# A decoder trunk on one core: the first tile's modulation split between TensorE and VectorE, its turned halves in two banks, the small rows turned later

## The chip, the cores and the metric

The kernel runs on one core of one Trainium2 chip. The metric is the device time of one execution in microseconds (us); three timed executions of the kernel before took 685.24, 685.53 and 686.24 us, so the median is 685.53 us.

## The reference

One decoder layer (`DEPTH = 1`) works on `x` of 512 rows by 1024 columns. What matters here is its head: a modulation is computed from a vector `c`, `x` is normalised and modulated, and the result is multiplied by the wide matrix `w_in`.

```python
cs = jax.nn.silu(c)
mod = cs @ w_ada[l] + b_ada[l]
shift1, scale1, gate1, shift2, scale2, gate2 = ...
h = _rmsnorm(x, norm1_g[l]) * (1.0 + scale1) + shift1
proj = h @ w_in[l]
qa, ka, va, qd, kd, vd, ga, gd = jnp.split(proj, points, axis=-1)
...
```

Behind it come a sliding-window attention, a differential attention, gates, an output projection and a gated MLP with a short convolution. All of that is the same in both kernels, in fp32 made of pairs of a rounded high part and a rest ("hi" and "lo").

## The kernel before, in words

**Layout.** `x` is held as `xn`, four tiles of 128 rows. `h` is needed transposed, as eight "k tiles" of 128 channels by 512 positions: `hTh[k]` (high part) and `hTl[k]` (rest). For every k tile the first stage needs a column pair `mods[k]` (scale and shift for 128 channels), which is a product of the vector `cs` with two 1024 by 128 slices of `w_ada` (`adaw[k]`, with `j` = 0 for the scale and 1 for the shift, and `kk` = 0..7 for the rows in groups of 128). It also needs 128 rows of `w_in` (768 columns, `w0[k]`), split into `w0h` and `w0l`. Six accumulators `acc6[0..5]`, one PSUM bank each, collect the products over the eight k tiles: per tile 6 x (`w0h` x `hTh`), 6 x (`w0l` x `hTh`) and 6 x (`w0h` x `hTl`).

**The head of the program.** `crow8` (the vector `c`) and `rows` (parts of `b_ada`, `norm1_g`, and `diff_subln_g`) are loaded and turned on TensorE; `rows` becomes `cols`, a column of biases and gains. TensorE runs filler products (`keep_warm(n)`: n blocks of 128 columns, products of ones with ones) while it waits. ScalarE squares the four tiles of `x` (`stat`), VectorE makes the reciprocal roots (`root`, which writes `rst`), the first 256 columns of each tile are scaled (`normalise` on VectorE for tiles 0 and 1, `scale_head` on ScalarE for 2 and 3), and `turn(t)` transposes the 128 columns of the first k tile into the bank `xt0`. Tile 0's modulation is summed from five products on TensorE (`direct0`, `kk` 0..4) and from three multiply-adds on VectorE (`add_a0`, `kk` 5..7, into `a0[j]`), which a last product with ones adds up. `finish_mod(0)` makes `mods[0]`; `h_tile(0)` writes `hTh[0]`, and the product of tile 0 begins.

**The eight tiles.** The loop over `gi` computes tile `gi`'s products on TensorE and, beside them, prepares tile `gi + 1`: `split_hi` on ScalarE, `ac_ops` on VectorE (the modulation sums), `reduce_mod`, `h_turn`, `finish_mod` (its shift column is written by ScalarE, line 337), `h_tile` on ScalarE (line 383: first `hTh`, then the same in fp32, `hf`), `h_low` on VectorE.

**What sets the order.** The loads of this stage lie in the SP queue in the order of the text: `x`, then `adaw` and `w0` of tile after tile, then four small loads (`sink`, `lamv`, `crow` twice), then the weights of the next stage: `w768_0`, `w1280_0` and so on, in 512 KB pieces (`load_cols`, line 567). Each engine runs its own instructions strictly in the order in which they are placed. Within `manual_schedule`, VectorE, ScalarE and TensorE keep the order of the text; instructions that are written behind that block are placed by a scheduler, by its own estimate of times, and it may put them in front of instructions of the block. Two such instructions of the next stage are the casts `w768_0_h` and `w1280_0_h` (line 128, `split`, called by `load_cols`), each 128 x 1024 on ScalarE.

Of the kernel before, what the change touches and what calls it, by code (L numbers as in the profile page):

```python
# [8 lines left out]
F32 = mybir.dt.float32  # L9
# [5 lines left out]
P = 128  # L15
D = 1024
S = 512
# [30 lines left out]
WARM_EARLY = 5  # L48
WARM = 8
# [11 lines left out]
def kernel(  # L61
# [104 lines left out]
    nc.sync.dma_start(crow8, c.rearrange("o (a p) -> (o a) p", p=P))  # L166
    NR = 16 + 8 + 1
# [3 lines left out]
    nc.scalar.dma_start(rows[24:25, :], diff_subln_g)  # L171
    crow = cpool.tile([88, P], F32, name="crow")
# [51 lines left out]
    def load_ada(k):  # L224
        if k % 3 == 2:
            aw = big.tile([P, 2, KT, P], F32, tag="out" + "hl"[k // 3], name=f"adaw{k}")
        else:
            aw = pp.tile([P, 2, KT, P], F32, tag="adaw", bufs=2, name=f"adaw{k}")
        cut = 4 if 0 < k < 5 else KT
        for a in range(0, KT, cut):  # L230
            for j, base in ((0, D), (1, 0)):
# [11 lines left out]
    with tc.manual_schedule(engines={nc.sync.engine}):  # L243
        for t in range(NT):
            nc.sync.dma_start(xn[:, t], xd[t * P : (t + 1) * P, :])
# [10 lines left out]
        nc.sync.dma_start(crow[66:88, :], conv_b[0].rearrange("(a p) -> a p", p=P))  # L256

# [10 lines left out]
    pc = tbank("pc", (P, NR))  # L268


    keep_warm(WARM_EARLY)
    nc.tensor.transpose(pc, rows, ident[:NR, :NR])
    cols = cpool.tile([P, NR], F32, name="cols")
    nc.vector.tensor_copy(cols, pc)
    bsh, bsc1, n1g, sublnc = cols[:, 0:8], cols[:, 8:16], cols[:, 16:24], cols[:, 24:25]
    nc.vector.tensor_scalar_add(bsc1, bsc1, 1.0)
    nc.vector.tensor_scalar_mul(n1g, n1g, -0.5)
    nc.vector.tensor_scalar_mul(sublnc, sublnc, -0.5 * (1.0 - LAM_INIT))
# [25 lines left out]
    def direct(pa, j, k, kks, start=True, stop=False):  # L304
        for kk in kks:
            nc.tensor.matmul(
                pa[:, j],
                adaw[k][:, j, kk],
                cs[:, kk : kk + 1].to_broadcast([P, P]),
                start=start and kk == kks[0],  # L310
                stop=stop and kk == kks[-1],
            )

    def early_mod(gi):
        pa = tbank(f"pa{gi}", (P, 2, P))
        direct(pa, 0, gi, (6, 7))
        return pa

    def reduce_mod(gi, early=None):
        pa = early or tbank(f"pa{gi}", (P, 2, P))  # L320
        for j in range(2):
            if early:
                if j:
                    direct(pa, 1, gi, (6, 7))
                nc.tensor.matmul(pa[:, j], ac[gi][0][:, j], ones, start=False, stop=True)
            else:
                nc.tensor.matmul(pa[:, j, 0:1], ac[gi][0][:, j], ones[:, 0:1], start=True, stop=True)
        return pa

    def finish_mod(k, pa):  # L330
        pa = pa if k == 0 else [pa[:, 0], pa[:, 1]]
        m = pp.tile([P, 16], F32, tag="mod", bufs=3, name=f"mod{k}")
        last = nc.vector.scalar_tensor_tensor(
            m[:, 0:1], pa[0][:, 0:1], bsc1[:, k : k + 1], n1g[:, k : k + 1], ALU.add, ALU.mult
        )
        if k:
            nc.scalar.activation(m[:, 1:2], pa[1][:, 0:1], AF.Identity, bias=bsh[:, k : k + 1])
        else:
            nc.vector.tensor_add(m[:, 1:2], pa[1][:, 0:1], bsh[:, k : k + 1])
        mods[k] = m  # L340
        return last
# [33 lines left out]
    def h_turn(k):  # L375
        pts[k] = tbank(f"xt{k}")
        for t in range(NT):
            nc.tensor.transpose(pts[k][:, t * P : (t + 1) * P], xn[:, t, k * P : (k + 1) * P], ident)

    def h_tile(k, between=None):  # L380
        hf = pp.tile([P, S], F32, tag="hf", bufs=2, name=f"hf{k}")
        for dst in (hTh[k], hf):
            nc.scalar.activation(dst, pts[k], AF.Identity, bias=mods[k][:, 1:2], scale=mods[k][:, 0:1])
# [11 lines left out]
    def mm_k(k, part, some=DONE):  # L395
# [4 lines left out]
        for i in some:  # L400
            for p in (1, 2) if last and part else (0, 1) if part == 0 and not last else (part,):
                lhs, rhs = ((wh, hTh), (wl, hTh), (wh, hTl))[p]
                nc.tensor.matmul(
                    acc6[i], lhs[:, i * P : (i + 1) * P], rhs[k], start=k == 0 and p == 0, stop=last and p == 2
                )
# [23 lines left out]
    pts[0] = tbank("xt0")  # L429

    def turn(t):
        nc.tensor.transpose(pts[0][:, t * P : (t + 1) * P], xn[:, t, 0:P], ident)
# [6 lines left out]
    DIRECT = 5  # L439

    def add_a0(j, kks):
        for kk in kks:
            w, f = adaw[0][:, j, kk], cs[:, kk : kk + 1]
            if kk == DIRECT:
# [4 lines left out]
    def direct0(j):  # L449
        for kk in range(DIRECT):  # L450
            nc.tensor.matmul(
                pa0[j], adaw[0][:, j, kk], cs[:, kk : kk + 1].to_broadcast([P, P]), start=kk == 0, stop=False
            )
# [16 lines left out]
    direct0(0)  # L470
    turn(2)
    direct0(1)
    for j in range(2):
        nc.tensor.matmul(pa0[j], a0[j], ones, start=False, stop=True)
    turn(3)
    finish_mod(0, pa0)
    split_hi(0, 0)
    keep_warm(2)
# [3 lines left out]
    for gi in range(KT):  # L482
# [20 lines left out]
        if gi == 0:  # L503
            h_turn(1)
        mm_k(gi, 0, DONE if gi else FIRST[:5])
        mm_k(gi, 1)
        if more:
            if gi == 0:
                split_lo(1, 0)
            pa = reduce_mod(gi + 1, early_mod(1) if gi == 0 else None)  # L510
            if gi == 0:
                mm_k(0, 0, FIRST[5:])
            if ALONE <= gi + 2 < KT:
# [5 lines left out]
            if gi:  # L519
                split_lo(gi + 1, 0)  # L520
# [38 lines left out]
    pcv = tbank("pcv", (P, 88))  # L559
    nc.tensor.transpose(pcv, crow, ident[:88, :88])  # L560
    cv = cpool.tile([P, P], F32, name="cv")
    nc.vector.tensor_copy(cv[:, :88], pcv)
# [1497 lines left out]
```

## Time and profile before

| what | value |
|---|---|
| median of three timed runs | 685.53 us (685.24 to 686.24) |
| profiled execution, first to last instruction (span) | 684.1 us |
| what lies around the span, against the median | 1.43 us |
| PE (TensorE) busy | 675.3 us, 99% |
| DVE (VectorE), ACT (ScalarE) busy | 564.2 us, 384.5 us |
| first product of tile 0 starts | 15.36 us |

The page gives the profiled execution's span; its own time, with the launch and the end around it, is not on the page, and is taken here as the span plus the 1.43 us by which the median exceeds it.

In the rows of a timeline, the first number is the start in us, the second the busy time in us, then the engine (PEld is TensorE's weight load, SPq the SP queue as it issues transfers), the line, the operation, output <- inputs, the shape and the count; brackets give the time for which the engine was idle before and what ended that. A row that holds several instructions starts with the first of them.

### The profile page before, as it was taken

What the parts mean: (1) busy time and instruction counts of PE and PEld (TensorE: products, weight loads), DVE (VectorE), ACT (ScalarE), POOL (GpSimd) and SP (SyncE); (2) the same over time, 40 slices, a digit from 0 to 9 for tenths busy, and PEclk for the clock granted to TensorE, in tenths of its full rate; (3) what the DMA queues carried; (4) which work ended last, traced back from release to release, by engine and by line L of the source; (5) the groups of instructions that cost most, each with busy time, mean ns of one, the idle gap of its engine ahead of it and who ended that gap; (6) DMA issues with size and microseconds to landing.
All of it is one profiled execution on the core that took longest, in us unless ns stands there. A gap on an engine that the chain in (4) does not pass through costs nothing. (4 is left out here: it accounts for less than half of the span.)

```text
span 684.1 us, 11125 instructions
## 1 busy us (share of the span) xinstructions
PE 675.3 (99%) x4141; PEld 589.7 (86%) x4141; DVE 564.2 (82%) x1075; ACT 384.5 (56%) x688; POOL 98.5 (14%) x119
## 2 busy tenths in 40 slices
PE   9999999999999999999999999999999999999995
PEld 5887887878888888888899999999999998888885
DVE  4999875988796756974589988888888999979997
ACT  6776774546543223324377665666555665656765
POOL 3000000011012012021030111112120003440300
PEclk9999999999999999999999999999999999999999
DMA  9995422565456885659555788777978647995903
GB/s 304 349 296 181 144 62 64 163 166 162 144 157 181 255 246 158 217 144 345 187 93 109 170 216 212 180 165 207 216 194 216 153 170 186 191 205 146 166 1 123
DMA packets 117142, 123.89 MB, mean 181 GB/s; under 512 B 5063, under 2 KB 94184, under 8 KB 117088
## 3 DMA queue, kind: packets, MB, share of 16 engines
q1 hardware_dynamic: 97246, 95.11, 43.3%
q0 software_dynamic: 19648, 27.79, 24.1%
q8 instruction: 32, 0.52, 0.3%
q10 hardware_dynamic: 194, 0.28, 0.1%
q14 instruction: 22, 0.18, 0.1%
HBM read 118.97 MB, written 2.11 MB: 177 GB/s over the span
## 5 line engine op out<-in xcount | busy, mean ns | idle before, releaser
L1362 PE MATMUL up<-t,m_whi 128*128 128x256 f32 x512 | 93.1, 283 | 0.0
L1362 PEld LDWEIGHTS up<-t,m_whi 128*128 128x128 f32 x512 | 79.9, 192 | 0.0
L1362 PE MATMUL up<-t,m_wlo 128*128 128x256 f32 x256 | 72.4, 283 | 0.0
L1362 PE MATMUL up<-bh,p_whi 128*128 128x256 f32 x232 | 65.7, 283 | 0.0
L1362 PE MATMUL up<-bl,p_whi 128*128 128x256 f32 x232 | 65.7, 283 | 0.0
L1362 PE MATMUL up<-bh,p_wlo 128*128 128x256 f32 x232 | 65.7, 283 | 0.0
L952 POOL DMA_DIRECT2D arow<-arow x28 | 22.5, 804 | 247.8 <-DVE sd L821 123.6
L1362 PEld LDWEIGHTS up<-t,m_wlo 128*128 128x128 f32 x256 | 49.2, 192 | 0.0
L1271 POOL DMA_DIRECT2D s<-in_w_up_dram x21 | 26.9, 1353 | 141.3 <-DMA s<-in_w_up_dram 69.2
L1362 PEld LDWEIGHTS up<-bh,p_whi 128*128 128x128 f32 x232 | 44.5, 192 | 0.0
L1362 PEld LDWEIGHTS up<-bl,p_whi 128*128 128x128 f32 x232 | 44.5, 192 | 0.0
L1362 PEld LDWEIGHTS up<-bh,p_wlo 128*128 128x128 f32 x232 | 44.5, 192 | 0.0
L944 DVE SCALAR_TENSOR_TENSOR arow<-ra,cs,arow 128x512 f32<-128x512 f32 x56 | 41.8, 748 | 0.6
L1299 ACT CAST m_whi<-s 128x1024 fp32r<-128x1024 f32 x31 | 32.4, 1046 | 11.1 <-DVE s L1293 6.3
L1303 DVE TENSOR_TENSOR m_wlo<-s,m_whi 128x1024 fp32r<-128x1024 f32 x31 | 37.8, 1218 | 0.0
L1362 PE MATMUL up<-t,p_whi 128*128 128x256 f32 x176 | 32.2, 283 | 0.0
L1362 PEld LDWEIGHTS up<-t,p_whi 128*128 128x128 f32 x176 | 27.5, 192 | 0.0
L816 ACT ACTIVATE sd<-sd,dmx 128x128 f32<-128x128 f32 (+3 forms) x32 | 17.7, 557 | 17.3 <-DVE dmx L806 17.3
L1369 ACT ACTIVATE gT<-a,cv 128x512 f32<-128x512 f32 x22 | 17.7, 813 | 16.9 <-DVE a L1404 15.8
L1299 ACT CAST p_whi<-wa 128x1024 fp32r<-128x1024 f32 x18 | 18.7, 1041 | 12.6 <-PE up L1362 12.6
L1303 DVE TENSOR_TENSOR p_wlo<-wa,p_whi 128x1024 fp32r<-128x1024 f32 x18 | 22.0, 1222 | 3.8 <-ACT p_whi L1299 3.8
L1362 PE MATMUL up<-t,p_wlo 128*128 128x256 f32 x88 | 24.9, 283 | 0.0
(499 smaller groups left out, 2052.4 us busy)
## 6 DMA issues: line engine op xcount, KB each, us to landing
ra<-in_w_ada_dram SPq DMA_DIRECT2D x32, 512.0 KB, 4.9
wa<-in_w_up_dram SPq DMA_DIRECT2D x22, 512.0 KB, 4.2
s<-in_w_up_dram SPq DMA_DIRECT2D x21, 512.0 KB, 4.7
s<-in_w_up_dram POOLq DMA_DIRECT2D x21, 512.0 KB, 6.9
w<-in_w_in_dram SPq DMA_DIRECT2D x12, 512.0 KB, 5.0
a<-in_w_up_dram SPq DMA_DIRECT2D x11, 512.0 KB, 4.7
b<-in_w_down_dram SPq DMA_DIRECT2D x10, 512.0 KB, 4.2
adaw<-in_w_ada_dram SPq DMA_DIRECT2D x8, 512.0 KB, 6.3
```

Of the source, the lines that this page charges most:

```text
L816: exp = nc.scalar.activation(pm[m], pm[m], AF.Exp, bias=mx[:, m : m + 1], scale=slope, accum_out=ls)
L944: nc.vector.scalar_tensor_tensor(ac, r[:, a], cc, ac, ALU.mult, ALU.add)
L952: nc.gpsimd.dma_start(whole[0:n], whole[n : 2 * n], accum_op=ALU.add)
L1271: nc.gpsimd.dma_start(dst, upblock(*blk), accum_op=ALU.add)
L1299: nc.scalar.copy(W[J, name][0], R[J, SRC[name]])
L1303: nc.vector.tensor_sub(lo, R[J, SRC[name]], hi.bitcast(F32))
L1362: nc.tensor.matmul(o[u], w[:, k, cu], b[:, k], start=name in ("p1", "m5", "p2") and k == 0 and x == 0, stop=k == 3 and x == 2, skip_group_ ...
L1369: nc.scalar.activation(grow(j), av[J][:, u], AF.Identity, bias=cv[:, 66 + j : 67 + j], scale=cv[:, 44 + j : 45 + j])
```

## The change

Seven edits, all in the first stage:

1. The load of `c` goes from the SP queue to ScalarE's queue, ahead of the small rows; `diff_subln_g` is no longer a row of `rows`; it is loaded behind `crow` by the SP queue and turned with `crow` (89 rows in place of 88).
2. `adaw[0]` is loaded in four pieces of 256 KB in place of two of 512 KB.
3. The filler products of 5 and 8 blocks (with the turn of `rows` between them) become one run of 25 blocks ahead of the first turn of `x`. The single block behind the second turn and the two blocks before the first product are gone.
4. `rows` is turned behind the second turn of `x` (`turn_rows`), into the bank of `acc6[3]`; VectorE's copy into `cols` stands ahead of `root(2)`.
5. Tile 0's modulation: TensorE takes `kk` 0..5 of the scale and 2..7 of the shift, VectorE the other two of each.
6. Tile 0's turned columns lie in two banks; VectorE writes the first half of `hTh[0]`, ScalarE the second.
7. In the products of tile 0, all `w0h` products come ahead of the `w0l` ones; the products for tile 1's modulation are put together and their sums placed behind the products of `acc6[5]`; `split_lo(1, 0)` moves behind `finish_mod(1)`.

```diff
-WARM_EARLY = 5
-WARM = 8
+WARM = 25
...
-    nc.sync.dma_start(crow8, c.rearrange("o (a p) -> (o a) p", p=P))
+    nc.scalar.dma_start(crow8, c.rearrange("o (a p) -> (o a) p", p=P))
...
-        cut = 4 if 0 < k < 5 else KT
+        cut = 4 if k < 5 else KT
...
+        nc.sync.dma_start(crow[88:89, :], diff_subln_g)
...
-    keep_warm(WARM_EARLY)
-    nc.tensor.transpose(pc, rows, ident[:NR, :NR])
...
+    def turn_rows():
+        pc = acc6[3][:, :NR]
+        nc.tensor.transpose(pc, rows, ident[:NR, :NR])
+        nc.vector.tensor_copy(cols, pc)
+        nc.vector.tensor_scalar_add(bsc1, bsc1, 1.0)
+        nc.vector.tensor_scalar_mul(n1g, n1g, -0.5)
...
         for dst in (hTh[k], hf):
-            nc.scalar.activation(dst, pts[k], AF.Identity, bias=mods[k][:, 1:2], scale=mods[k][:, 0:1])
+            for src in pts[k]:
+                q = slice(src[1], src[1] + src[0].shape[-1])
+                if k == 0 and dst is not hf and src[1] == 0:
+                    nc.vector.tensor_scalar(dst[:, q], src[0], mods[k][:, 0:1], mods[k][:, 1:2], ALU.mult, ALU.add)
+                else:
+                    nc.scalar.activation(
+                        dst[:, q], src[0], AF.Identity, bias=mods[k][:, 1:2], scale=mods[k][:, 0:1]
+                    )
...
         if t in (1, 2):
             normalise(t - 1)
             turn(t - 1)
-            keep_warm((4, 1)[t - 1])
+            if t == 1:
+                keep_warm(4)
+                direct0(0, range(4), True)
+    turn_rows()
     root(2)
-    add_a0(0, range(DIRECT, DIRECT + 2))
+    add_a0(0, (6,), 6)
     root(3)
-    add_a0(0, range(DIRECT + 2, KT))
-    add_a0(1, range(DIRECT, KT))
+    add_a0(0, (7,), 6)
+    add_a0(1, (0, 1), 0)
     scale_x(0)
     scale_head(2)
     scale_head(3)
     scale_x(1)
-    direct0(0)
+    direct0(0, (4, 5))
+    direct0(1, (2, 3), True)
     turn(2)
-    direct0(1)
-    for j in range(2):
-        nc.tensor.matmul(pa0[j], a0[j], ones, start=False, stop=True)
+    sum0(0)
     turn(3)
-    finish_mod(0, pa0)
+    direct0(1, range(4, KT))
+    sum0(1)
...
-    keep_warm(2)
+    h_turn(1)
```

Where the instructions stand changes in the head, as the text says, and in one place that the text doesn't show.

TensorE in the head, from the filler products (`a5<-ones`) to the last products of tile 0's modulation; before, from the filler run to the first five products of the scale:

```order
L184 MATMUL a5_113<-ones_67 128x512
L184 MATMUL a5_113<-ones_67 128x128
L272 MATMUL pc_193<-ident_69,rows_103 128x25
L184 MATMUL a5_113<-ones_67 128x512 x2
L432 MATMUL xt0_205<-ident_69,xn_123 128x128
L184 MATMUL a5_113<-ones_67 128x512
L432 MATMUL xt0_205<-ident_69,xn_123 128x128
L184 MATMUL a5_113<-ones_67 128x128
L451 MATMUL pa0_206<-cs_188,adaw0_130 128x128 x5
```

and in the changed kernel:

```order
L182 MATMUL a5_112<-ones_67 128x512 x6
L182 MATMUL a5_112<-ones_67 128x128
L441 MATMUL xt0_204<-ident_69,xn_122 128x128
L182 MATMUL a5_112<-ones_67 128x512
L459 MATMUL pa0_205<-cs_190,adaw0_129 128x128 x4
L441 MATMUL xt0_204<-ident_69,xn_122 128x128
L275 MATMUL a3_114<-ident_69,rows_103 128x24
L459 MATMUL pa0_205<-cs_190,adaw0_129 128x128 x2
L459 MATMUL a4_110<-cs_190,adaw0_129 128x128 x2
L441 MATMUL a5_112<-ident_69,xn_122 128x128
L465 MATMUL pa0_205<-ones_67,a0_0_206 128x128
L441 MATMUL a5_112<-ident_69,xn_122 128x128
```

Ahead of the first turn of `xn` stand 25 filler blocks without a break in place of 13 with the turn of `rows` in them, and the turn of `rows` now follows the second turn of `xn`, behind four products of the modulation.

ScalarE near the end of the first stage, from the last part of tile 7's modulation (`ac7`) over tile 6's shift column and transposed tile (`mod6`, `hThB`) to those of tile 7; `w768_0_h` and `w1280_0_h` are the casts of the next stage's weights. Before:

```order
L288 ACTIVATE ac7_0_579<-adaw7_173,cs_188 128x256
L337 ACTIVATE mod6_586<-pa6_574,cols_197 128x1
L383 ACTIVATE hThB_117<-xt6_581,mod6_586 128x512
L383 ACTIVATE hf6_591<-xt6_581,mod6_586 128x512
L361 CAST w0h7_600<-w0_7_176 128x512
L363 CAST w0h7_600<-w0_7_176 128x256
L128 CAST w768_0_h_706<-w768_0_704 128x1024
L128 CAST w1280_0_h_712<-w1280_0_710 128x1024
L337 ACTIVATE mod7_632<-pa7_624,cols_197 128x1
```

and in the changed kernel:

```order
L289 ACTIVATE ac7_0_582<-adaw7_174,cs_190 128x256
L127 CAST w768_0_h_710<-w768_0_708 128x1024
L337 ACTIVATE mod6_589<-pa6_577,cols_195 128x1
L386 ACTIVATE hThB_116<-xt6_584,mod6_589 128x512
L386 ACTIVATE hf6_594<-xt6_584,mod6_589 128x512
L358 CAST w0h7_603<-w0_7_177 128x512
L360 CAST w0h7_603<-w0_7_177 128x256
L127 CAST w1280_0_h_716<-w1280_0_714 128x1024
L337 ACTIVATE mod7_635<-pa7_627,cols_195 128x1
```

The cast of `w768_0` has moved from behind tile 7's casts to ahead of tile 6's shift column; `w1280_0`'s keeps its place. Behind this stage the order of every engine is the same in both kernels, but for the bias column's new name and its one scaling on VectorE.

More of the change, by code (lines that the diff above doesn't have):

```diff
@@ L311, in direct @@
                 stop=stop and kk == kks[-1],
+                skip_group_check=True,
             )
@@ L315, in early_mod @@
         pa = tbank(f"pa{gi}", (P, 2, P))
-        direct(pa, 0, gi, (6, 7))
+        for j in range(2):
+            direct(pa, j, gi, (6, 7), start=j == 0)
         return pa
@@ L328, in reduce_mod, with mod_scale @@
         return pa
+    def mod_scale(k, pa):
+        m = mods[k] = pp.tile([P, 16], F32, tag="mod", bufs=3, name=f"mod{k}")
+        return nc.vector.scalar_tensor_tensor(m[:, 0:1], pa, bsc1[:, k : k + 1], n1g[:, k : k + 1], ALU.add, ALU.mult)
     def finish_mod(k, pa):
[L331 to L340, printed above, removed]
+        last = mod_scale(k, pa[:, 0, 0:1])
+        nc.scalar.activation(mods[k][:, 1:2], pa[:, 1, 0:1], AF.Identity, bias=bsh[:, k : k + 1])
         return last
@@ L399, in mm_k @@
             return
[L400 to L405, printed above, removed]
+        ps_ = (1, 2) if last and part else (0, 1) if part == 0 and not last else (part,)
+        order = [(i, p) for i in some for p in ps_]
+        if k == 0:
+            order.sort(key=lambda e: e[1])
+        for i, p in order:
+            lhs, rhs = ((wh, hTh), (wl, hTh), (wh, hTl))[p]
+            nc.tensor.matmul(
+                acc6[i], lhs[:, i * P : (i + 1) * P], rhs[k], start=k == 0 and p == 0, stop=last and p == 2
+            )
     keep_warm(WARM)
```

68 lines of the change are left out of this document (34 added, 34 removed).

## The prediction

> **What bounds the kernel now.** I read the page first, then the timeline of TensorE (PE) over the head and over the last two tiles of the first stage, then ScalarE (ACT), VectorE (DVE) and the SP queue at the same places.
>
> ```profile
> span 684.1 us, 11125 instructions
> PE 675.3 (99%) x4141; PEld 589.7 (86%) x4141; DVE 564.2 (82%) x1075; ACT 384.5 (56%) x688; POOL 98.5 (14%) x119
> ```
>
> TensorE is busy nearly throughout, so the time moves by what TensorE waits in this stage, and by nothing else that the change touches: behind the stage the instructions stand in the same order. 0.2% of 685.53 us, 1.37 us, is about what a measurement of this kernel can tell from no change.
>
> The head, on TensorE:
>
> ```profile
> 3.04 2.50 PE L184 MATMUL a<-ones 128*128 128x512 f32 x4
> 5.70 3.78 PE L184 MATMUL a<-ones 128*128 128x512 f32 x4
> 8.42 1.06 PE L184 MATMUL a<-ones 128*128 128x512 f32 x1
> 9.28 0.34 PE L432 MATMUL xt<-ident,xn 128*128 128x128 f32 x1
> 9.45 1.02 PE L184 MATMUL a<-ones 128*128 128x512 f32 x2
> 10.31 0.29 PE L432 MATMUL xt<-ident,xn 128*128 128x128 f32 x1
> 10.85 1.38 PE L451 MATMUL pa<-cs,adaw 128*128 128x128 f32 x10
> 12.07 0.27 PE L432 MATMUL xt<-ident,xn 128*128 128x128 f32 x1
> 13.85 0.39 PE L474 MATMUL a<-ones,a 128*128 128x128 f32 x2
> 15.36 0.50 PE L403 MATMUL a<-hThA,w0h 128*128 128x512 f32 x1
> ```
>
> The starts tell the clock. One pass of 512 columns takes 0.85 us at 8.42 (to the turn at 9.28), but two take 0.86 us at 9.45 (to 10.31). So TensorE runs at half speed until about 9.4 us, 3.7 us after the unbroken filler began at 5.70. A block of 128 columns is two passes of 128: 0.43 us slow, 0.215 us fast.
>
> The end of the stage, first on TensorE, then on ScalarE:
>
> ```profile
> 44.51 1.64 PE L403 MATMUL a<-hTlA,w0h 128*128 128x512 f32 x6
> 45.98 0.39 PE L403 MATMUL a<-hThB,w0h 128*128 128x512 f32 x1
> ...
> 50.24 0.84 PE L403 MATMUL a<-hTlB,w0h 128*128 128x512 f32 x3
> 51.27 0.74 PE L403 MATMUL a<-hThB,w0h 128*128 128x512 f32 x2 [0.19 <-ACT hThB L383]
> ```
>
> ```profile
> 44.55 0.26 ACT L337 ACTIVATE mod<-pa,cols 128x1 f32<-128x1 f32 x1 [0.92 <-DVE mod L333]
> 44.86 0.78 ACT L383 ACTIVATE hThB<-xt,mod 128x512 fp32r<-128x512 f32 x1
> ...
> 46.71 0.41 ACT L363 CAST w0h<-w 128x256 fp32r<-128x256 f32 x1
> 47.58 1.05 ACT L128 CAST w_h<-w 128x1024 fp32r<-128x1024 f32 x1 [0.46 <-DMA w<-in_w_in_dram]
> 49.20 1.05 ACT L128 CAST w_h<-w 128x1024 fp32r<-128x1024 f32 x1 [0.57 <-DMA w<-in_w_in_dram]
> 50.15 0.25 ACT L337 ACTIVATE mod<-pa,cols 128x1 f32<-128x1 f32 x1
> 50.44 0.78 ACT L383 ACTIVATE hThB<-xt,mod 128x512 fp32r<-128x512 f32 x1
> ```
>
> Both casts of the next stage's weights start when their load lands, at 47.58 and 49.20. The second already costs TensorE something: tile 7's shift column stands behind it, so `hThB` begins at 50.44, and the product that reads it at 51.27. The three products at 50.24 are 0.23 us apart, so without that wait it would have begun at 50.92: 0.35 us lost. Tile 6's shift column, at 44.55, has no cast ahead of it.
>
> **The change part by part.** *The moved cast.* In the changed kernel the cast of `w768_0` stands ahead of tile 6's shift column. Its load is far down the SP queue:
>
> ```profile
> 0.74 0.40 SPq L166 DMA_DIRECT2D crow<-in_c_dram  x1
> 1.20 1.78 SPq L245 DMA_DIRECT2D xn<-in_x_dram  x4
> ...
> 41.06 0.35 SPq L256 DMA_DIRECT2D crow<-in_conv_b_dram  x1
> 41.46 3.62 SPq L567 DMA_DIRECT2D w<-in_w_in_dram  x3
> ```
>
> ```profile
> L567 SPq DMA_DIRECT2D w<-in_w_in_dram x5: 368/420/2372, 41.5 to 51.6; - x5
> ...
> DMA to landing us min/median/max: 6.1/6.5/7.0
> ```
>
> ```profile
> 20.00:25.00 5.00, 5.00 (x27) 4.23 (x26) 4.24 (x11) 4.58 (x10) 0.00 (x0) 1.00 1.11 360
> 35.00:40.00 5.00, 5.00 (x28) 4.26 (x27) 4.59 (x12) 3.39 (x8) 0.00 (x0) 1.00 1.05 313
> ```
>
> In the windows' last two columns, the engines of the transfers are full (share above 1, 313 to 360 GB/s) from 20 to 40 us: the queue runs at the pace of the transfers and not of the compute, so a later compute doesn't make the load later, nor an earlier one earlier. The load of `c` leaves this queue, so `x` and all behind it start 0.46 us earlier (1.20 less 0.74); the load of `diff_subln_g` puts one more issue, 0.40 us (41.06 to 41.46), ahead of `w768_0`. The issue is then at 41.46 - 0.46 + 0.40 = 41.40, and 6.1 us on the load lands at about 47.5. If instead the whole stream of transfers is 0.46 us ahead, it lands at 47.58 - 0.46 = 47.1. I take 47.3.
>
> From there the path is ScalarE's own: cast to next instruction 0.95 (49.20 to 50.15), shift column 0.29 (50.15 to 50.44), `hThB` to TensorE's product 0.83 (50.44 to 51.27). 47.3 + 0.95 + 0.29 + 0.83 = 49.37, against 45.98 before: 3.39 us later. TensorE is strictly behind it: the next product in its order reads `hThB`. VectorE isn't delayed in itself, its next step for tile 6 reads `hf`, which ScalarE writes behind `hThB`. The wait at tile 7 goes: ScalarE gets through `hf` and tile 7's casts 2.26 us after `hThB` began (44.86 to 46.71 + 0.41), so by 50.8, and through `w1280_0` by 51.8; tile 7's product isn't reached before 49.37 + 4.94 = 54.3 (45.98 to 50.92). That returns 0.35 us. Net +3.04 us.
>
> The Trainium skill, page DMA: Bandwidth & Descriptors, section Anatomy of one DMA, fits 2.0 us plus bytes at 436 GB/s for a transfer of the other path; by it, as an estimate, 512 KB would land 3.2 us after issue, at 44.6, and the sum would be that of the second case below, 687.1. The trace has 6.1 to 7.0 us for these loads, so the row decides.
>
> *The head.* 25 filler blocks run from 3.04 ahead of the first turn. If the clock opens 3.7 us after the unbroken run begins, as above, it opens at 6.74; 8.6 blocks are done then, and 16.4 more take 3.5 us: the first turn comes at 10.3, not 9.28. The bounds are 8.4 (25 x 0.215, fast from the start) and 13.8 (25 x 0.43, slow throughout). Behind it on TensorE come the turn (0.17), four blocks (0.86), eight passes of the modulation (0.12 each by the ten from 10.85 to 12.07, 0.96), a turn (0.12) and the turn of `rows` (0.3): 12.7. VectorE's copy into `cols` waits for that, and the roots of `x` tiles 2 and 3 are queued behind the copy:
>
> ```profile
> 5.81 0.18 DVE L274 COPY cols<-pc 128x25 f32<-128x25 f32 x1 [1.67 <-PE pc L272]
> 6.25 0.15 DVE L191 TENSOR_SCALAR ms<-ss 128x1 f32<-128x1 f32 x1
> 10.64 0.21 DVE L201 SCALAR_TENSOR_TENSOR rt<-r,ms 128x1 f32<-128x1 f32 x1
> 11.31 0.35 DVE L447 SCALAR_TENSOR_TENSOR a<-adaw,cs,a 128x128 f32<-128x128 f32 x1
> 11.58 0.21 DVE L201 SCALAR_TENSOR_TENSOR rt<-r,ms 128x1 f32<-128x1 f32 x1
> 11.82 0.16 DVE L205 SCALAR_TENSOR_TENSOR rst<-rt,r 128x1 f32<-128x1 f32 x1
> 14.28 0.16 DVE L339 TENSOR_TENSOR mod<-a,cols 128x1 f32<-128x1 f32 x1
> ```
>
> ```profile
> 12.08 0.51 ACT L427 ACTIVATE xn<-xn,rst 128x256 f32<-128x256 f32 x1 [0.31 <-DVE rst L205]
> 14.53 0.78 ACT L383 ACTIVATE hThA<-xt,mod 128x512 fp32r<-128x512 f32 x1 [0.59 <-DVE mod L339]
> ```
>
> Copy and two scalings take about 0.37 (5.81 to 6.25, less one small one), so `root(2)` comes at 13.1 instead of 10.64. From there to the last root is 0.91 (10.64 to 11.82, less the one multiply-add that moves, 11.31 to 11.58): 14.0. ScalarE's scaling follows 0.26 later and takes 0.51: 14.8. Then the last turn and eight passes on TensorE (1.1): 15.9; sum to `mods[0]` 0.43 + 0.1: 16.4; to the transposed half 0.25, the half itself 0.51 (the 128 x 256 row, for the 0.78 of the whole): 17.1. So tile 0's product starts at about 17.0, 1.6 us later than 15.36. With the bounds of the filler it is 15.1 to 20.5, near the low end by the 3.7 us seen.
>
> This 1.6 us isn't added. It makes tile 6's shift column wanted at 46.15 instead of 44.55, and the cast ahead of it ends later still. The place of the wait sets the time, and the head's loss lies inside it.
>
> The Trainium skill, page TensorE: Matmul & The Clock Gate, section Part 1: The HAM clock gate, says that the gate looks at free-running windows of 3.4 us, so that the opening may come anywhere from one to two windows after steady work begins. The trace's 3.7 us agrees; as an estimate that would spread the opening over 6.5 to 9.9 us and tile 0's first product over about 16.9 to 18.6, all of it still inside the wait.
>
> *At nothing:* the load of `c` on the other queue (its issue was the first there too, at 0.74), `adaw[0]` in four pieces (same bytes), the split of `hf[0]` (ScalarE, beside 2.3 us of products), the 89th column. The order of tile 1's sums may cost 0.1 to 0.2 us of TensorE at tile 1, and that too lies inside the wait.
>
> **The rivals.** *Second case, the cast finds its load there:* then the head decides, +1.6 us, less nothing, 687.1 us; 686.8 to 688.6 with the spread of the opening. For it: ScalarE is idle 0.92 us before 44.55, into which a cast of 0.95 would fit. Against it: the load landed 3 us after that point, and the queue is full ahead of it. It decides if the load lands before about 45.2. Chance 0.12.
>
> *Third, the other side:* the filler is fast from the start, and the load is there. Then `x` is 0.46 us earlier and the half transposed tile saves 0.27 (0.78 less 0.51), at most 0.7 us, and 0.35 more if the wait at tile 7 goes: 684.5 to 684.8 us, not slower, and not outside 0.2% either. It decides if the clock opens before about 4 us. Against it: at 5.70 to 9.28 the filler ran at half speed. Chance 0.04.
>
> *Fourth, the clock closes again:* TensorE has done its work for tile 5 at about 47.6 (45.98 + 1.6) and idles until 49.4. No row shows that 1.8 us of idle time closes the clock; if it did, 3.7 us at half speed would cost another 1.85 us, 690.4. Chance 0.04.
>
> **How the numbers follow.** The forecast has the other 0.80. Its span is 684.1 + 3.04 = 687.14, and what lies around the span is 1.43 us against the median, or 1.14 against the fastest run (685.24): 688.57 or 688.28. I take 688.4. A load that lands 1.1 us later (7.0 us after 41.40, the slowest of the row) gives 689.6; an end 1.5 us below comes with the load near 45.8, where the second case takes over. The range is 686.9 to 689.6. All of the forecast, the fourth case and half of the second are slower by over 0.2%: 0.90. The rest of the second and most of the third are within it: 0.08. Faster by over 0.2% gets 0.02.
>
> **What would show it.** Right: on ScalarE, the first cast of `w_h` with an idle time ended by its load, then tile 6's shift column directly behind it, near 48.3; on TensorE an idle time of over 1 us ended by ScalarE's `hThB`, tile 6's first product near 49.4, and no wait at tile 7. The head: 25 blocks ending near 10.3, tile 0's first product near 17. Wrong: the cast starts without a wait, or tile 6's first product lies less than 2 us behind 45.98.

## The result, and the profile after

The changed kernel took 693.54 us (median of six executions, 690.18 to 695.72), the kernel before 685.76 beside it: a ratio of 1.0115, 95% interval 1.0093 to 1.0137. It is slower, as forecast, but by 7.8 us where 2.9 were forecast, and outside the range of 686.9 to 689.6. The profiled execution took 693.41 us.

The page's first rows of the changed kernel, which answer to the first two of the prediction:

```profile
span 691.6 us, 11138 instructions
...
PE 679.1 (98%) x4147; PEld 591.3 (85%) x4147; DVE 563.0 (81%) x1074; ACT 384.2 (56%) x689; POOL 98.4 (14%) x119
```

The span grew by 7.5 us, and TensorE's busy time by 3.8: half of the loss is idle time. Of the 3.8 us, 1.1 lie ahead of tile 0's first product (15.0 us busy there in place of 13.9), and 1.6 are products at half speed, which come below. The timeline of TensorE over the head:

```profile
3.03 7.46 PE L182 MATMUL a<-ones 128*128 128x512 f32 x14
10.33 0.27 PE L441 MATMUL xt<-ident,xn 128*128 128x128 f32 x1
...
12.40 0.24 PE L275 MATMUL a<-ident,rows 24*128 24x24 f32 x1
...
16.99 0.47 PE L411 MATMUL a<-hThA,w0h 128*128 128x512 f32 x1 [0.48 <-ACT hThA L386]
```

The first turn came at 10.33 and tile 0's first product at 16.99, where the working had 10.3 and 17.0. VectorE and ScalarE show the chain that the prediction named: the copy into `cols` waits for the turn of `rows`, and ScalarE's scaling for the roots behind that copy.

```profile
12.67 0.18 DVE L276 COPY cols<-a 128x24 f32<-128x24 f32 x1 [2.82 <-PE a L275]
```

```profile
13.48 1.09 ACT L435 ACTIVATE xn<-xn,rst 128x256 f32<-128x256 f32 x2 [3.00 <-DVE rst L203]
```

The end of the stage, on ScalarE and on TensorE:

```profile
48.59 1.04 ACT L127 CAST w_h<-w 128x1024 fp32r<-128x1024 f32 x1 [2.37 <-DMA w<-in_w_in_dram]
49.55 0.26 ACT L337 ACTIVATE mod<-pa,cols 128x1 f32<-128x1 f32 x1
49.83 0.78 ACT L386 ACTIVATE hThB<-xt,mod 128x512 fp32r<-128x512 f32 x1
```

```profile
46.98 1.64 PE L411 MATMUL a<-hTlA,w0h 128*128 128x512 f32 x6
50.66 0.50 PE L411 MATMUL a<-hThB,w0h 128*128 128x512 f32 x1 [2.04 <-ACT hThB L386]
51.00 0.52 PE L411 MATMUL a<-hThB,w0l 128*128 128x512 f32 x1
51.32 0.63 PE L411 MATMUL a<-hThB,w0h 128*128 128x512 f32 x1
51.75 0.63 PE L411 MATMUL a<-hThB,w0l 128*128 128x512 f32 x1
...
54.31 0.50 PE L411 MATMUL a<-hThB,w0l 128*128 128x512 f32 x1
...
57.33 1.56 PE L411 MATMUL a<-hThB,w0h 128*128 128x512 f32 x6
```

The cast waits for its load, the shift column stands directly behind it, and TensorE waits 2.04 us for `hThB`: this is the forecast's picture, 1.29 us later than its 49.37. Behind the wait the products are 0.43 us apart and not 0.23. The stage's windows show why, and show something else that the prediction had not expected (the last three columns are the granted clock, the transfers' share and their GB/s):

```profile
20.00:25.00 5.00, 4.97 (x26) 3.88 (x25) 4.38 (x11) 3.47 (x8) 0.00 (x0) 1.00 1.18 318
35.00:40.00 5.00, 5.00 (x27) 4.20 (x26) 4.55 (x12) 3.32 (x7) 0.00 (x0) 1.00 1.15 316
...
50.00:55.00 5.00, 4.33 (x12) 3.42 (x13) 1.41 (x3) 3.04 (x5) 0.00 (x0) 0.66 0.95 272
```

The clock closed: 0.66 is a mean, and the trace's clock record has half speed from 51.11 to 54.53 us, 3.413 us long. And from 20 to 25 us the transfers moved 318 GB/s with a share of 1.18, where the kernel before moved 360 with 1.11. In the trace's single records a packet of 512 bytes took 27 ns before (nearly all of them exactly so) and 30 to 34 in the mean of any 2.5 us from 7.5 us on after (most between 27 and 40). More time for fewer bytes: the transfers themselves had become slower, through the whole stage.

Set against the kernel before, TensorE's delay grows along the program like this: 1.63 us at tile 0's first product (15.36 to 16.99), 2.40 at tile 2's sums (23.73 to 26.13), 4.68 at tile 6 (45.98 to 50.66), 6.28 at the end of the half clock (48.02 to 54.31), 6.06 at tile 7 (51.27 to 57.33), 6.27 at 248, 7.43 at 305, and 7.4 to 7.6 from there to the end. The rows of tile 2's sums, before and after:

```profile
23.73 0.50 PE L327 MATMUL pa<-ones,ac 128*128 128x1 f32 x4
```

```profile
26.13 0.58 PE L328 MATMUL pa<-ones,ac 128*128 128x1 f32 x4 [0.33 <-DVE ac L302]
```

The step at 305 us is far behind the change. The waits of TensorE, in us, times, longest, name it:

```profile
PE a L411 <- ACT hThB L386: 2.0, 1, 2.0
...
PE pB L133 <- DVE wbd L128: 0.9, 1, 0.9
```

### The profile page after: what moved, and what is told of

Read it like the earlier page. It is cut to its first block, busy times and chain, and to the rows that moved or that the text cites. A ratio compares the mean times of both kernels' runs of the same rounds, so it can differ in the third digit from the quotient of the medians.

```text
span 691.6 us, 11138 instructions
## 1 busy us (share of the span) xinstructions
PE 679.1 (98%) x4147; PEld 591.3 (85%) x4147; DVE 563.0 (81%) x1074; ACT 384.2 (56%) x689; POOL 98.4 (14%) x119
## 5 line engine op out<-in xcount | busy, mean ns | idle before, releaser
L968 POOL DMA_DIRECT2D arow<-arow x28 | 22.5, 803 | 261.8 <-DVE sd L837 130.5
L1378 PEld LDWEIGHTS up<-t,p_whi 128*128 128x128 f32 x176 | 27.5, 192 | 0.0
```

The source lines that it names most:

```text
L968: nc.gpsimd.dma_start(whole[0:n], whole[n : 2 * n], accum_op=ALU.add)
L1378: nc.tensor.matmul(o[u], w[:, k, cu], b[:, k], start=name in ("p1", "m5", "p2") and k == 0 and x == 0, stop=k == 3 and x == 2, skip_group_ ...
```

## The experiments

In the first two groups the kernel before took 685.43 us beside them, in the third 685.98, then 685.50 and 685.53; differences below are against the one of the same group. "Packets" are the 512-byte packets of the first 57 us, by the mean of their times.

**Is it the moved cast?** *e1* holds both casts behind tile 7's, where the kernel before has them.

```diff
-            nc.scalar.copy(wts[k][0][:, 512:768], w0[k][:, 512:768])
+            return nc.scalar.copy(wts[k][0][:, 512:768], w0[k][:, 512:768])
...
-            split_hi(gi + 1)
+            last_act = split_hi(gi + 1)
...
-    with tc.issue_after(last_mod.ins):
+    with tc.issue_after(last_mod.ins), tc.issue_after(last_act.ins):
```

> The changed kernel with one thing undone: the casts of w768_0 and w1280_0 stand on ScalarE behind tile 7's casts again, as in the kernel before. Theory A (the moved cast): of the 7.5 us between the two profiles, tile 6's wait, the half clock behind it and the later row sums all hang on the cast's place, and only the head and the short waits at tiles 1 and 2 (2.4 us by the product of tile 3) are left: about 688.2 us, 687.4 to 689, clock at full speed at tile 6. Theory B (slower transfers): the small packets of the first 50 us, 32 ns each for 27, delay the stage whatever stands ahead of what: over 690 us, and TensorE still waits over 1 us at tile 6 or 7.

689.01 us (+3.6; ratio 1.0053, 1.0038 to 1.0068). The wait at tile 6, the half clock and the wait for `wbd` are all gone; TensorE is 1.93 us late at tile 0, 2.73 at tile 2, and 2.43 from tile 7 to the end. So in the changed kernel the cast's place costs 4.5 us, with what follows from it. But the rest is larger than the head's forecast 1.6, and the packets stay at 32 ns.

*e2* adds a shorter filler, `WARM = 13`.

> The same with 13 filler blocks ahead of the first turn in place of 25. Theory A: the filler ends near 8.7 to 9.3 us instead of 10.3, so everything behind it in the head comes 1 to 1.6 us earlier, tile 0's first product at 15.4 to 16.0: 685.8 to 687 us. Theory B: no change against the run with 25 blocks, since a transfer sets when tile 0 can begin: within 0.4 us of it.

688.32 us (+2.9). Tile 0's first product came 1.2 us earlier than in e1 (16.11), but by tile 4 TensorE was 2.85 us late again: there it waits 1.15 us for `hThA`, ahead of which ScalarE had waited 2.61 us for the load of `adaw`. What the head gains, slower loads take back.

**Is it the clock?** *e3* keeps the changed kernel's order and lets TensorE add products with zeros to `acc6[3]` ahead of tile 6's first product, so that it is not idle there.

```diff
+FILL = 2
...
+        if gi == 5:
+            for _ in range(FILL):
+                nc.tensor.matmul(acc6[3], zeros, ones4, start=False, stop=False, skip_group_check=True)
```

> The changed kernel with its cast in the new place and two products of 512 columns by zeros (added to an accumulator, 1.7 us of TensorE) behind tile 5's last product, in the idle time ahead of tile 6. Theory A1 (idle time closes the clock): no stretch of half speed behind tile 6's wait, 1.6 us less: 691.5 to 692.3 us where the changed kernel takes 693.5, and tile 6's products at 0.23 us each from the first on. Theory A2 (the clock closes for another reason, or by chance): a stretch of 3.4 us at half speed as in the changed kernel, no gain against it.

692.9 us in the median, above the 692.3 of theory A1; of four executions two took near 691 and two near 695. The profiled one is the slowest (695.2). In it the clock opened only at 9.47 us, and tile 0's first product was 3.13 us late in place of 1.63. At tile 6 TensorE is kept busy and the clock stays open, but later TensorE waits 2.09 us for weights, and there it closes:

```profile
50.01 1.88 PE L543 MATMUL a<-ones,zeros 128*128 128x512 f32 x4
51.32 0.79 PE L414 MATMUL a<-hThB,w0h 128*128 128x512 f32 x1
51.95 0.40 PE L414 MATMUL a<-hThB,w0l 128*128 128x512 f32 x1
...
339.36 0.50 PE L1441 MATMUL oc<-wo_wlo,mg3h 128*128 128x512 f32 x1 [2.09 <-DVE wo_wlo L129]
...
341.14 0.63 PE L1441 MATMUL oc<-wo_wlo,mg3h 128*128 128x512 f32 x1
```

So the median can't price the half clock at tile 6; the profile shows that it is gone there, and that a late stream of weights can find another place.

*e4* takes the five small loads out of the SP queue, so that `w768_0` might be issued earlier, and keeps the cast where the change has it.

```diff
-        nc.sync.dma_start(sink, swa_sinks[0].partition_broadcast(P))
+        nc.gpsimd.dma_start(sink, swa_sinks[0].partition_broadcast(P))
```

(and so for `lamv` and the three of `crow`; `w1280_0`'s cast is held as in e1.)

> The changed kernel with w768_0's cast in its new place, ahead of tile 6's shift column, but the five small loads (sink, lamv, crow three times) taken out of the SP queue and issued by GpSimd at the start, so that w768_0's load is issued about 2 us earlier. Theory A: the cast finds its load or waits less than 0.6 us, and what is left is the head: 688 to 689.3 us, no half clock. Theory C (the cast costs by its own 0.95 us ahead of the shift column, not by its load): tile 6 is still 1 us or more late, 689.5 us or more.

692.83 us, and the load did not come earlier. The SP queue and ScalarE of e4:

```profile
40.76 2.89 SPq L241 DMA_DIRECT2D w<-in_w_in_dram  x1
43.70 4.38 SPq L583 DMA_DIRECT2D w<-in_w_in_dram  x3
```

```profile
50.08 1.04 ACT L127 CAST w_h<-w 128x1024 fp32r<-128x1024 f32 x1 [1.84 <-DMA w<-in_w_in_dram]
```

The issue of `w768_0` starts at 43.70, as in the changed kernel (43.67), where five issues stood ahead of it: here the queue's time was not the sum of its issues, it waited for the transfers ahead. TensorE waits 2.03 us at tile 6 here too, and the clock stays open (1.00 from 50 to 55 us).

The clock records tell the two waits apart. In every trace here, all changes of the clock lie whole multiples of 3.413 us behind its first opening (in the changed kernel the closing 13 of them, at 51.11). The stretch that ends with that closing, and the two of e4 on which its wait falls, have these rows (the second number is TensorE's busy time):

```profile
47.70:51.11 3.41, 1.37 (x6) 0.80 (x6) 3.02 (x8) 2.48 (x4) 0.00 (x0) 1.00 1.14 295
```

```profile
47.14:50.55 3.41, 2.98 (x18) 2.23 (x16) 3.00 (x9) 1.38 (x3) 0.00 (x0) 1.00 1.11 292
50.55:53.96 3.41, 1.81 (x8) 1.52 (x9) 2.35 (x6) 3.38 (x7) 0.00 (x0) 1.00 1.11 323
```

The changed kernel's wait lies whole in one stretch, 2.04 us idle; e4's is cut in two, 0.4 and 1.6 us. The other closings ahead of the program's end fit: TensorE idled 2.09 us in the stretch ahead of e3's, 1.61 and 1.67 us ahead of one in the head of e5 and of e8 (the two runs below), and in no stretch that left the clock open did it idle longer than e4's 1.6. So what decides in these traces is the idle time within one stretch, about 1.6 us of it (the ends of products are modelled, so no sharper limit is shown), and with it where the wait falls.

**Which part makes the transfers slow?** Three runs take the edits that touch loads. *e5* is e2 with `adaw[0]` in two pieces again, *e6* the kernel before with the four pieces alone, *e7* the kernel before with the load of `c` on ScalarE's queue alone.

```diff
-        cut = 4 if k < 5 else KT
+        cut = 4 if 0 < k < 5 else KT
```

> The changed kernel with the casts behind tile 7's and 13 filler blocks (as in e2), and adaw[0] loaded again in two pieces of 512 KB. Theory B1 (the four pieces of adaw[0] make the packets of the first 57 us slow): 512-byte packets back at 27 ns in place of 32, the late wait at tile 3 to 4 of e2 (2.85 us behind the kernel before at 38.9 us) gone, first product of tile 0 near 16.1, time 688.3 less 1.3 to 2 us, so 686.3 to 687. Theory B2 (c's load on ScalarE's queue, or x starting 0.46 us earlier, does it): packets stay at 32 ns and the time at 688.3.

> The kernel before with one part of the change alone: adaw[0] in four pieces of 256 KB. No instruction of an engine moves. Theory B1 (the four pieces): 512-byte packets 32 ns in place of 27 in the first 57 us, the rate from 10 to 30 us falls from about 360 to 313 GB/s, and TensorE waits for loads at tiles 2 to 4: +1 to +2.7 us, 686.5 to 688.2. Theory B2 (c's load): 27 ns and 685.4, as the kernel before.

> The kernel before with one other part alone: the load of c on ScalarE's queue, ahead of the small rows; x starts some 0.46 us earlier on the SP queue. Theory B1 (the four pieces slow the transfers): packets 27 ns, time within 0.5 us of the kernel before, 685.0 to 685.9. Theory B2 (the load of c, or the earlier x): packets 32 ns, 686.5 to 688.2.

e5: 689.11 us, packets 32 ns (in its profile TensorE waits 1.7 us for `adaw[0]`, and the clock is at half speed again from 13.07 to 16.49 us). e6: 685.36 (1.0003, 0.9994 to 1.0012), 27 ns. e7: 687.0 (1.0020, 1.0011 to 1.0029), 27 ns. The window from 20 to 25 us of e5, e6 and e7, in that order:

```profile
20.00:25.00 5.00, 4.97 (x29) 3.98 (x27) 4.36 (x11) 3.48 (x8) 0.00 (x0) 1.00 1.17 314
```

```profile
20.00:25.00 5.00, 5.00 (x28) 4.22 (x27) 4.28 (x10) 4.58 (x10) 0.00 (x0) 1.00 1.11 361
```

```profile
20.00:25.00 5.00, 5.00 (x27) 4.18 (x26) 4.56 (x12) 3.97 (x8) 0.00 (x0) 1.00 1.12 358
```

Neither edit is the cause; both theories fell. (e7's 1.6 us have another reason, as far as its one profile tells: the small rows now wait behind `c` on ScalarE's queue, TensorE's turn of `rows` at 6.67 waits 0.92 us for `diff_subln_g`, the filler is broken there, and the clock opens late, at 12.38.)

*e8* looks at the prediction's 0.35 us at tile 7: the kernel before with both casts behind `hf[7]`.

> The kernel before with both casts of the next stage's weights held behind tile 7's transposed tile (hf). The prediction's reading of the trace before says that tile 7's first product loses 0.35 us to the cast of w1280_0 ahead of its shift column: by it 685.4 - 0.35 = 685.1, if the casts, one us later, are not wanted earlier by the next stage. Rival: the first product of the next stage reads these casts, and waits for them: 685.4 or up to 1 us more.

686.01 us (1.0006, 0.9993 to 1.0019): nothing gained. The profile is of the slowest of its ten executions (688.2 us; the clock closed in its head, from 12.13 to 15.55). In it the wait at tile 7 is gone, and one of the same size stands at the next stage's first product:

```profile
57.89 0.50 PE L132 MATMUL pq<-hThA,w_h 128*128 128x512 f32 x1 [0.35 <-DVE qa L541]
```

**The buffers' places.** All kernels made from the changed one had slow packets, all made from the one before had not, whatever their loads did. What they share is the layout of SBUF. `cols` has one column less (`diff_subln_g` is no longer in it): 24 x 4 = 96 bytes in each partition in place of 100. Room is given in steps of 32 bytes, so it takes 96 in place of 128, and every buffer that is placed behind it lies 32 bytes lower. `adaw[0]` starts at byte 169984 of each partition before and at 169952 after, `xn` at 153600 and 153568, the buffer of `w768_0` at 120832 and 120800. Two runs change only this: *f1* is the changed kernel with the column back, unused; *f2* is the kernel before with 7 more.

```diff
-    cols = cpool.tile([P, NR], F32, name="cols")
+    cols = cpool.tile([P, NR + 1], F32, name="cols")[:, :NR]
```

> The changed kernel with one column of padding behind cols (25 columns allocated, 24 used), and nothing else: every engine's instructions stand as in the changed kernel, but all buffers behind cols in SBUF lie where the kernel before has them, at multiples of 64 bytes, and not 32 bytes lower. Theory D (the 32 bytes make the loads' packets slow): 512-byte packets back at 27 ns, 10 to 30 us at some 355 GB/s in place of 313, w768_0 lands at about 47.3 us in place of 48.6, tile 6's first product comes near 49.4, the time near the forecast of 688.4, or 690.0 if the clock still closes at tile 6. Theory E (the changed order of the loads, or c on the other queue, makes them slow): packets stay at 32 ns, time 693.

> The kernel before with 7 more columns allocated behind cols (132 bytes in place of 100) and nothing else: every instruction as before, all buffers behind cols 32 bytes higher, off the multiples of 64 bytes. Theory D: packets at 32 ns, 10 to 30 us at some 313 GB/s, TensorE waits for loads in the first stage, the cast of w1280_0 stands later ahead of tile 7's shift column: +1.5 to +4 us, 687 to 689.5. Theory E: 27 ns and 685.4.

f1: 687.99 us (+2.0; 1.0033, 1.0021 to 1.0044), packets 27.5 ns. f2: 688.36 us (+2.4; 1.0037, 1.0023 to 1.0050), 31 ns. Theory D holds from both sides: one unused column is worth 5.8 us to the changed kernel, and 32 bytes cost the kernel before 2.4. The window of f1, then that of f2:

```profile
20.00:25.00 5.00, 4.98 (x27) 3.94 (x26) 4.36 (x12) 3.48 (x9) 0.00 (x0) 1.00 1.13 359
```

```profile
20.00:25.00 5.00, 4.75 (x23) 3.61 (x22) 4.17 (x10) 4.25 (x8) 0.00 (x0) 1.00 1.14 313
```

In f2, whose instructions are those of the kernel before, the slow loads reach TensorE over ScalarE's part of the modulation sums:

```profile
36.68 0.91 ACT L288 ACTIVATE ac<-adaw,cs 128x256 f32<-128x256 f32 x2 [2.61 <-DMA adaw<-in_w_ada_dram]
```

```profile
38.60 0.50 PE L403 MATMUL a<-hThA,w0h 128*128 128x512 f32 x1 [1.46 <-ACT hThA L383]
```

And in f1 the moved cast is all but free. Its SP queue, ScalarE and TensorE:

```profile
41.14 3.73 SPq L583 DMA_DIRECT2D w<-in_w_in_dram  x3
```

```profile
46.44 1.05 ACT L127 CAST w_h<-w 128x1024 fp32r<-128x1024 f32 x1 [0.81 <-DMA w<-in_w_in_dram]
47.39 0.26 ACT L337 ACTIVATE mod<-pa,cols 128x1 f32<-128x1 f32 x1
```

```profile
47.22 1.63 PE L411 MATMUL a<-hTlA,w0h 128*128 128x512 f32 x6
48.69 0.40 PE L411 MATMUL a<-hThB,w0h 128*128 128x512 f32 x1
```

The cast still waits for its load, but TensorE is already 2.71 us late at tile 2's sums and stays exactly so at tile 6: no idle time.

*f3* and *f4* are e1 and e2 with the column.

> e1 (the changed kernel with both casts behind tile 7's, as in the kernel before) with the column of padding. Theory D: the waits of tiles 1 and 2 and those of e1 go, the head's 1.6 us stay: 685.4 + 1.6 = 687.0, against 689.0 of e1. The difference to f1 is then what the moved cast costs at a full rate of transfers, 1.4 us by the prediction (3.04 less 1.6), or 3 if the clock closes. Theory E: 689.0.

> e2 (casts back, 13 filler blocks) with the column of padding. Theory D: the late waits of e2 go, and the head decides: first product of tile 0 near 16.1 against 15.36, so 685.4 + 0.75 = 686.1, less 0.35 if the wait at tile 7 is gone: 685.8. If the clock opens early enough, the split modulation and the earlier x win, down to 684.8. Theory E: 688.3.

f3: 688.19 us (+2.2; 1.0035, 1.0021 to 1.0048), the same as f1 within the spread: at the full rate, and behind a head this late, the moved cast costs nothing measurable. f4: 686.35 (+0.4; 1.0007, 0.9999 to 1.0016): 12 filler blocks fewer are worth 1.84 us. f3 missed its 687.0 by 1.2, since the head is not all that is late (below).

**Which places are slow, and what is left.** *g1*, *h1*, *h2* and *h3* are the kernel before with all buffers behind `cols` 64, 128, 256 and 512 bytes higher, by `NR + 16`, `+ 32`, `+ 64` and `+ 128` columns.

> The kernel before with 16 more columns allocated behind cols (164 bytes, 192 with the rounding, in place of 100 and 128) and nothing else: all buffers behind cols 64 bytes higher, again at multiples of 64 bytes. Theory D1 (it is the multiple of 64 bytes that counts): packets 27 ns, time as the kernel before, 685.2 to 686.2. Theory D2 (any other place of the buffers, or the multiple of 128 bytes, is slow): packets 30 to 32 ns, 688.4 as f2.

> The kernel before with all buffers behind cols 128 bytes higher. In the kernel before, the loads' targets begin at multiples of 1024 bytes, and adaw's 512-byte packets at multiples of 512. Theory D3 (a packet has to begin at a multiple of 512 bytes, its own size): 32 ns and 688.4. D4 (a multiple of 128 is enough): 27 ns, 685.5. D5 (only the very place of before is fast, by some other buffer's place): 32 ns, 688.4, here and at 256 and 512 bytes.

> The kernel before with all buffers behind cols 256 bytes higher. D3 (multiple of 512): 32 ns and 688.4. D4 (128), or a multiple of 256: 27 ns, 685.5. D5: 32 ns, 688.4.

> The kernel before with all buffers behind cols 512 bytes higher. D3 and D4: 27 ns, 685.5. D5 (only the very place of before): 32 ns, 688.4.

| buffers moved by | time, us | ratio and interval | packets, mean of 20 to 22.5 us | GB/s, 20 to 25 us |
|---|---|---|---|---|
| 32 bytes (f2) | 688.36 | 1.0037, 1.0023 to 1.0050 | 30.0 ns | 313 |
| 64 (g1) | 688.44 | 1.0047, 1.0031 to 1.0062 | 30.2 ns | 313 |
| 128 (h1) | 688.35 | 1.0041, 1.0022 to 1.0059 | 32.8 ns | 312 |
| 256 (h2) | 685.12 | 0.9994, 0.9980 to 1.0008 | 27.2 ns | 333 |
| 512 (h3) | 685.54 | 1.0000, 0.9986 to 1.0015 | 27.0 ns | 357 |

The windows of h1 and of h2:

```profile
20.00:25.00 5.00, 5.00 (x26) 4.26 (x27) 4.21 (x11) 3.44 (x9) 0.00 (x0) 1.00 1.16 312
```

```profile
20.00:25.00 5.00, 5.00 (x28) 4.23 (x27) 4.40 (x11) 4.71 (x10) 0.00 (x0) 1.00 1.06 333
```

My first guess, a multiple of 64 bytes, fell with g1, and the packet's own size with h2: of the places tried, multiples of 256 bytes are fast, and nothing less is. (h2's lower GB/s is not slow packets: its share fell with it.) The Trainium skill, page DMA: Bandwidth & Descriptors, section How a descriptor splits into AXI transactions, has this rule: pieces of 256 bytes that have to start at multiples of 256, so that a descriptor of 512 bytes that starts elsewhere needs three in place of two. The page tells it of reading; these runs moved the written side alone, and agree: 313 in place of 360 GB/s. That the extra piece is what costs the time is argued: no trace here shows the pieces.

*g3* is f4 with two more parts undone: `rows` is turned behind the first turn of `x`, and `split_lo(1, 0)` stands ahead of tile 1's sums again.

```diff
             if t == 1:
+                turn_rows()
                 keep_warm(4)
...
-    turn_rows()
     root(2)
...
             if gi == 0:
+                split_lo(1, 0)
                 early = early_mod(1)
...
-            split_lo(gi + 1, 0)
+            if gi:
+                split_lo(gi + 1, 0)
```

> f4 (13 filler blocks, casts behind tile 7's, the column of padding) with two more parts of the change undone: rows is turned behind the first turn of x and not the second, so that VectorE's copy into cols stands ahead of the third root and not of it and the fourth; and split_lo(1, 0) stands ahead of tile 1's sums again. In f4 the first cost tile 0's first product about 0.4 us and the second 0.6 us at tile 2's sums (0.33 us of them in one wait). If both go: first product of tile 0 at 15.2, tile 2's sums at the place of the kernel before, 686.35 - 0.9 = 685.4, at most 0.6 us faster than the kernel before. Rival: the clock's opening, which differs from execution to execution, sets the first product, and it stays at 686.0.

684.60 us against 685.50 (ratio 0.9986, 0.9978 to 0.9995): faster than both kernels, by a little. TensorE's rows of f4 show what stood there, and those of g3 that it is gone:

```profile
15.57 1.39 PE L411 MATMUL a<-hThA,w0h 128*128 128x512 f32 x5 [0.49 <-ACT hThA L386]
...
24.69 0.58 PE L328 MATMUL pa<-ones,ac 128*128 128x1 f32 x4 [0.33 <-DVE ac L302]
```

```profile
14.98 1.38 PE L411 MATMUL a<-hThA,w0h 128*128 128x512 f32 x5 [0.48 <-ACT hThA L386]
...
23.61 0.50 PE L328 MATMUL pa<-ones,ac 128*128 128x1 f32 x4
```

Tile 0's first product is 0.38 us earlier than in the kernel before, and tile 2's sums don't wait. But the head's gain is gone soon after: from tile 3 on TensorE is 0.2 us behind the kernel before, and it is ahead to the end, by 0.3, because tile 7's wait is gone too.

## Why the prediction was right or wrong

**The head: right in its steps, lucky in its number.** Filler to 10.3, first product at 17.0, by the steps named; the clock opened at 6.74 us in the clock record, as worked out. But the 3.7 us from filler to opening hold for no rule: in the six kernels with this filler the profiled execution opened the clock between 6.05 (f3) and 9.47 (e3), and tile 0's first product came between 16.6 and 18.5. f2, with the instructions of the kernel before, opened it at 4.90, ahead of the 5.70 from which the 3.7 us were counted. The spread that the prediction gave beside its sum, 6.5 to 9.9 us, covers four of the six.

**The order of tile 1's sums, "0.1 to 0.2 us": too small.** Between tiles 0 and 2 the delay grew by 0.77 us (1.63 to 2.40), and by 0.75 in f1. `split_lo(1, 0)` behind `finish_mod(1)` puts 0.68 us of VectorE ahead of tile 2's sums; before, it stood in a gap. With g3's order the wait is gone.

**The landing of `w768_0`, 47.3 us: the step that failed.** It rested on the sentence that four pieces, another queue and one column more cost nothing, and on the queue's running at the transfers' pace, which was read from the kernel before and taken as fixed. The first holds for the pieces and the queue (e6, and e7's packets); the list leaves out that `cols` got narrower. The pace itself changed: the column that went out of `cols` moved the targets of nearly all loads off the multiples of 256 bytes; the issue came at 43.67 and not 41.40, the cast at 48.59. At the old pace (f1) they are 41.14 and 46.44. From issue to cast that is 4.9 and 5.3 us, where I took 6.1. The Trainium skill, page DMA: Bandwidth & Descriptors, section Anatomy of one DMA, gives 3.2 us for 512 KB of the other path, as an estimate; the measured times lie between the two, nearer to the 6.1.

**The moved cast, +3.04 us: right in mechanism, wrong in its condition.** All of it is seen in the changed kernel: cast, shift column, `hThB`, no wait at tile 7. But "the place of the wait sets the time" holds only while the load is late against the head. At the old pace the shift column is wanted at 44.55 + 2.71 = 47.26 and the cast has to start by 46.3; it starts at 46.44, and TensorE doesn't wait. So my second case (0.12), not the forecast (0.80), is what the change would have done had the buffers stayed, although the load landed at 46.4 and not before the 45.2 that I had set for it. In f1's profile tile 0 is 1.96 us late and tile 1's order adds 0.75, with 0.4 back at tile 7: 2.3 us, and 687.99 where the case had 687.1. That this is near the forecast's 688.4 is chance: the working to it is not what happened in either kernel.

**The fourth case (0.04), the clock closing in the wait: it happened.** Price 1.85 us forecast, 1.60 seen (4.68 to 6.28). I had no row for it and counted that as evidence against. Given that a wait of about 2 us was itself the forecast, an unknown price of this size belonged in the range. Whether it closes depends on how the wait lies in the stretches of 3.413 us: with the same 2.0 us it did in the profile of the changed kernel and did not in e4. That the changed kernel's times spread over 5.5 us fits this, but was not shown.

**"By nothing else that the change touches": wrong at the end.** 1.16 us were lost at 305 us, where the load of `wbd` was issued at 285.26 in place of 273.94. In the SP queue it stands behind a load that waits for the transfer into `mod_rows`, longer than before; the queue's waits after, then before:

```profile
SPq L1153 <- DMA mod_rows<-arow: 11.1, 1, 11.1
```

```profile
SPq L1137 <- DMA mod_rows<-arow: 6.2, 1, 6.2
```

In e1 that wait is 6.4 us and in e4 6.6, and neither loses time at this place, though e4's TensorE is as late at tile 7 as the changed kernel's (5.95 us for 6.06). So a late first stage alone doesn't cause it, and why that transfer came late in the changed kernel stays open.

The sum of the changed kernel's own trace: 1.63 (head) + 0.77 (tile 1's order) + 2.28 (wait for the cast) + 1.60 (half clock) - 0.22 (tile 7) + 0.21 + 1.16 (later stages) = 7.43 of 7.5 us. Against the 3.04 us of the prediction that is 4.39 more: 1.29 for the later landing, 1.60 for the clock, 1.37 in later stages, and 0.13 that tile 7 gave back less. By the runs: 5.8 us of the 7.8 go with the column (+7.8 to f1's +2.0), 1.6 with the 12 filler blocks and the cast's place (f1 to f4; the blocks alone, f3 to f4, 1.84), and the last 0.4 are within what g3 takes back.

Small slips in the prediction's numbers change nothing: 688.4 and 1.1 are 689.5, not 689.6, and around the span lie 1.7 to 1.9 us in every execution on record, not 1.43.

## What to carry to other kernels

A tile that becomes smaller or larger moves every buffer behind it, without a line of the order changing: after such an edit look at the buffers' addresses, and keep the targets of loads at multiples of 256 bytes (here an unused column was enough). When a profile's transfers move fewer GB/s at a higher share, look at the buffers' places as well as at the order. And when a forecast makes TensorE wait about 2 us, price a closing clock with it, as a chance and not as a certainty.

## What the runs showed of the hardware that I had not expected

- The place of a load's target sets its speed: 512-byte packets took 27 ns in the mean at multiples of 256 bytes and 31 to 32 at 32, 64 and 128 beside them; from 20 to 25 us the loads fell from 360 to 313 GB/s.
- TensorE's clock changed only at whole multiples of 3.413 us from its first opening, in all 19 traces. Inside a run it closed four times, each time at the end of a stretch of that length in which TensorE idled 1.61 to 2.09 us, and opened again 3.413 us later; with 1.6 us at most it stayed open (e4). The Trainium skill, page TensorE: Matmul & The Clock Gate, section Part 1: The HAM clock gate, gives free-running windows of this length, which agrees with the 3.413 us, and one idle window of it for the closing, which doesn't: a window idle for 1.61 us of it was enough.
- Issues that were taken out of a full queue did not bring the next one forward: 43.70 in e4 against 43.67 with five more ahead.
